# One attention job for both heads of a pair, and score and state products that alternate between row halves

## The chip, the core and the metric

One core of a Trainium2 chip runs the whole program. The metric is the device time of one execution in microseconds (us). TensorE (PE) does the matrix products from on-chip memory into the PSUM banks; VectorE (DVE), ScalarE (ACT) and GpSimd (POOL) do everything else; SyncE (SP) issues most transfers. Each engine runs its own instructions in the order in which the program wrote them, and engines wait for each other by semaphores.

## The reference, cut to what matters

Two decoder layers over 256 tokens and a width of 2048. Each layer projects the input, runs four groups of heads side by side (A: an RWKV-7 recurrence; B: stick-breaking attention; C: dilated window attention; D: differential attention), projects back, and then does a SwiGLU feed-forward block.

```
for l in range(DEPTH):
    p = h @ w_proj
    y_a = rwkv7_time_mix(r_a, k_a, v_a, ...)          # 8 heads of 64, a scan over tokens
    y_b = stick_breaking_attention(q_b, k_b, v_b)     # 8 heads of 64
    y_c = dilated_attention(q_c, k_c, v_c, rel_tab_c) # 8 heads of 64
    y_d = differential_attention(q_d, k_d, v_d, ...)  # 4 heads, each with two score maps of 64
    x = x + g1 * (concat(y_a, y_b, y_c, y_d) @ w_out[l])
    x = x + g2 * swiglu(adaLN(x))
```

In B and C a score map is `q @ k^T` with 64 terms per sum, over two blocks of 128 queries; in D each head has two such maps, subtracted after their softmax. In A the recurrence is computed in 8 chunks of 32 tokens; each chunk needs products of a running state with the chunk's rows.

## The kernel before

The program is written out once, by a planner in Python. The big projections run as "quads": weights come in by DMA as `raw`, ScalarE rounds them to `hi`, VectorE makes the rest `lo = raw - hi`, and each weight tile takes three products (`hi` with `hh`, `hi` with `hl`, `lo` with `hh`). After every few products of a quad the planner calls `tick`, which lets the jobs that are due write some instructions. So the PE queue is a stream of projection products into which pieces of attention and of the recurrence are put, and it is fixed when the program is built.

Attention jobs are Python generators that give way at each `yield`. In B (`stick`) and C (`dilated`) there is one job per head, 8 per group and layer; at most `width` = 3 of them are open at once. In D (`diff`) there is one job per head, up to 4 open, and it makes its two score maps one after the other. Two heads, 2j and 2j+1, share a tile: `q[j]` and `k[j]` hold head 2j in partitions 0 to 63 and head 2j+1 in partitions 64 to 127, so the two heads' score products use the two halves of TensorE's rows. `scores` makes one head's map with a product of 128 queries by 128 keys and one of 128 by 256. These products are in fp32, and the profile shows two records for each.

All small products write into four PSUM banks (`P`, names `m...`). A job takes banks with `bank` and gives them back to the planner with `drop` when the instructions that read them are written; in the run, the next writer of a bank waits for a semaphore until they are done. The recurrence (`rwkv`, higher priority) holds two banks, `XY`, for four chunks at a time, and takes one more for each of its other products. In each chunk but the first `state_part` is called twice: eight products with 64 rows, four for `e` = 0 (partitions 0 to 63, bank `XY[0]`) and four for `e` = 1 (partitions 64 to 127, bank `XY[1]`).

All instructions go through one helper, so the profile puts them on L180; tile names tell them apart: `qk` the q and k tiles, `S` with `kq` the state products, `aT` with `v` the value products, `consts` with `be` or `e` the transposes of the attention matrix, `sa`, `TT`, `tm` and `ab` the other products of the recurrence, and `q<-...` the projections.

Of the kernel before, what the change touches and what calls it, by code (L numbers as in the profile page):

```python
# [10 lines left out]
AF = mybir.ActivationFunctionType  # L11
ALU = mybir.AluOpType
# [12 lines left out]
NEG = -1e30  # L25
# [143 lines left out]
class Engine:  # L169


    def __init__(self, k, name, eng):
        self.k, self.ename, self.eng = k, name, eng
# [22 lines left out]


class Job:
    def __init__(self, gen, ready=0.0, prio=5):
        self.gen, self.ready, self.prio = gen, ready, prio  # L200
        self.t0 = self.made = ready


# [7 lines left out]
class Kern:  # L211
# [120 lines left out]
    def C(self, name):  # L332
        o, w = CONST[name]
        return self.consts[:, o:o + w]
# [149 lines left out]
    def tick(self, force=False):  # L484
        if self.lows and self.lows[0][5] <= self.clock["tensor"] + self.cfg.get("la", 0):
            self.lower()
        self.ada_pump()
        now = self.clock["tensor"]
        while sum(j.prio == 5 for j in self.active) < self.width and self.jobs:
            self.active.append(self.jobs.popleft())  # L490
            self.active[-1].t0 = now
        for j in list(self.active):
            if j.ready <= now and (j.prio < 2 or force or max(self.clock["vector"], self.clock["scalar"]) < now + self.cfg.get("jg", 1e9)):
                if not self.step(j):
                    self.active.remove(j)
        if force:
            self.clock["tensor"] += 200.0

    def add(self, g, prio=5):
        j = Job(g, self.clock["tensor"], prio)  # L500
        if prio < 5:
            self.active.append(j)
            self.active.sort(key=lambda x: x.prio)
        else:
            self.jobs.append(j)
# [436 lines left out]
    def rwkv(self, l, A):  # L942
        nc = self.nc
        C = self.C
        tt, stt = nc.vector.tensor_tensor, nc.vector.scalar_tensor_tensor
        lo, k, v = A["lo"], A["k"], A["v"]
# [25 lines left out]
        pss = yield from self.bank()  # L972
# [54 lines left out]
        for c in range(8):  # L1027
# [4 lines left out]
                sa0, sa = self.T2(n="sa0"), self.T2(n="sa")  # L1032

            def state_part(col, which, Sx):
                for e in range(2):
                    es = slice(64 * e, 64 * e + 64)
                    for j in range(4):
                        nc.tensor.matmul(XY[e][P, col + j * 64:col + j * 64 + 64], kq[j][es, c, which, :],
                                         Sx[es, j * 64:j * 64 + 64], start=j == 0, stop=False, skip_group_check=True)

# [114 lines left out]
                self.ys[j] = R["yo"][j]  # L1155


    def scores(self, G, h, ps):
        j, e = divmod(h, 2)
        es = slice(64 * e, 64 * e + 64)  # L1160
        q, k = G["q"][j], G["k"][j]
        self.nc.tensor.matmul(ps[:, 0:128], q[es, 0:128], k[es, 0:128], start=True, stop=True)
        self.nc.tensor.matmul(ps[:, 128:384], q[es, 128:256], k[es, 0:256], start=True, stop=True)

    def transposed(self, att3):

# [5 lines left out]
    def A3(self, n):  # L1172
        return self.T2(n=n)[:, 0:384]

    def attend(self, G, h, aT, base):

        nc = self.nc
        G["aT"][h] = aT
        if h ^ 1 not in G["aT"]:
            return  # L1180
        j = h // 2
        o = yield from self.bank()
        for e in range(2):
            aT = G["aT"].pop(2 * j + e)
            es = slice(64 * e, 64 * e + 64)
            vs = slice((2 * j + e) * 64, (2 * j + e) * 64 + 64)
            nc.tensor.matmul(o[es, 0:256], G["v"][0][:, vs], aT[:, 0:256], start=True, stop=False)
            nc.tensor.matmul(o[es, 128:256], G["v"][1][:, vs], aT[:, 256:384], start=False, stop=True)
# [5 lines left out]
    def stick(self, G, h):  # L1194
        nc = self.nc
        C = self.C
        ps = yield from self.bank()
        self.scores(G, h, ps)
        om, be = (self.T2(n=n)[:, 0:387] for n in ("om", "be"))
        nc.gpsimd.memset(om[:, 128:387:258], 0.0)  # L1200
        nc.gpsimd.memset(om[:, 257:258], 1.0)
        om3 = om.rearrange("p (b k) -> p b k", k=129)
        be3 = be.rearrange("p (b k) -> p b k", k=129)
        ps3 = ps[:, 0:384].rearrange("p (b k) -> p b k", k=128)
        nc.scalar.activation(om3[:, :, 0:128], ps3, AF.Sigmoid, scale=-1.0)
        nc.scalar.activation(be3[:, :, 0:128], ps3, AF.Sigmoid)
        self.drop()
        yield
        for t3, fill in ((om3, 1.0), (be3, 0.0)):
            d = t3[:, 0:3:2, 0:128]  # L1210
            nc.gpsimd.affine_select(d, d, [[0, 2], [-1, 128]], ALU.is_gt, fill, base=0, channel_multiplier=1)
        yield
        nc.vector.tensor_tensor_scan(om[:, ::-1], om[:, ::-1], C("sent")[:, ::-1], 1.0, ALU.mult, ALU.add)

        s1 = bass.AP(tensor=om.tensor, offset=om.offset + 1, ap=[list(om.ap[0]), [129, 3], [1, 128]])
        nc.vector.tensor_tensor(be3[:, :, 0:128], be3[:, :, 0:128], s1, ALU.mult)
        yield
        att3 = be3[:, :, 0:128]
        pt = yield from self.transposed(att3)
        aT = self.A3("aT")  # L1220
        nc.scalar.activation(aT[:], pt[:, 0:384], AF.Copy)
        self.drop()
        yield
        yield from self.attend(G, h, aT, 4)

    def load_bias(self, hb):
        t = self.T(n="bias")
# [5 lines left out]
    def softmax_parts(self, ps, bt):  # L1233

        nc = self.nc
        e = self.A3("e")
        m, s = self.small(2, "m"), self.small(2, "sm")
        for b, (a0, a1, b0) in enumerate(((0, 128, 128), (128, 384, 0))):
            nc.vector.tensor_tensor_reduce(e[:, a0:a1], ps[:, a0:a1], bt[:, b0:256], 1.0, 2 * NEG, ALU.add, ALU.max,
                                           m[:, b:b + 1])  # L1240
        nc.vector.tensor_scalar(m, m, -1.0, None, ALU.mult)
        self.drop()
        yield
        for b, (a0, a1) in enumerate(((0, 128), (128, 384))):
            nc.scalar.activation(e[:, a0:a1], e[:, a0:a1], AF.Exp, bias=m[:, b:b + 1], accum_out=s[:, b:b + 1])
        yield
        nc.vector.reciprocal(s, s)
        return e, s

    def scaled(self, a, s, key, l):  # L1250
        if self.cfg.get(key, 0) & (1 << l):
# [1 line left out]
        else:  # L1253
            self.nc.vector.tensor_scalar(a, a, s, None, ALU.mult)

    def dilated(self, l, G, h):
        nc = self.nc
        bt = self.load_bias(h)
        yield
        ps = yield from self.bank()  # L1260
        self.scores(G, h, ps)
        e, s = yield from self.softmax_parts(ps, bt)
        for b, (a0, a1) in enumerate(((0, 128), (128, 384))):
            self.scaled(e[:, a0:a1], s[:, b:b + 1], "na", l)
        yield
        pt = yield from self.transposed(e[:].rearrange("p (b k) -> p b k", k=128))
        aT = self.A3("aT")
        nc.scalar.activation(aT[:], pt[:, 0:384], AF.Copy)
        self.drop()
        yield  # L1270
        yield from self.attend(G, h, aT, 8)

    def diff(self, l, G, h):
        nc = self.nc
        es = []
        bt = self.load_bias(8 + h)
        yield
        for c in range(2):
            ps = yield from self.bank()
            self.scores(G, 2 * h + c, ps)  # L1280
            es.append((yield from self.softmax_parts(ps, bt)))
        (e0, s0), (e1, s1) = es
        nc.vector.tensor_scalar(s1, s1, self.lam[:, l:l + 1], None, ALU.mult)
        for b, (a0, a1) in enumerate(((0, 128), (128, 384))):
            self.scaled(e1[:, a0:a1], s1[:, b:b + 1], "nd", l)
# [136 lines left out]
    def layer(self, l, rstd):  # L1422
# [47 lines left out]
        for g in GROUPS:  # L1470
# [14 lines left out]
            def evv(q, G, g, sp=None):  # L1485
                for hf in range(2):
                    t = self.T2(n="v")
                    if sp:
                        nc.vector.tensor_tensor(t[:], q[hf], sp[hf][:], ALU.add)
                    else:  # L1490
                        nc.scalar.activation(t[:], q[hf], AF.Copy)
                    G["v"].append(t)
                    yield
                if g == "B":
                    for h in range(8):
                        self.add(self.stick(G, h))
                elif g == "C":
                    for h in range(8):
                        self.add(self.dilated(l, G, h))
                else:  # L1500
                    self.width = self.cfg.get("dw", 4)
                    for h in range(4):
                        self.add(self.diff(l, G, h))
            q = self.quad("q" + g, hs, "ch")
# [301 lines left out]
```

## Time and profile before

| | |
|---|---|
| time, median of 3 runs | 2706.76 us (2697.99 to 2708.77) |
| the profiled execution's own time | 2684.77 us |
| its span in the trace | 2683.1 us |
| TensorE busy | 2617.4 us, 98% of the span |
| VectorE, ScalarE busy | 67%, 42% |
| attention and recurrence, layer 0 | about 270 to 545 us of the span |
| attention and recurrence, layer 1 | about 1585 to 1870 us |

The profile is of one execution. A record of TensorE lasts from its start until its result is out, so records that follow each other overlap; what one piece of work costs the PE queue is read from its start to the start of the next piece.

### The profile page before, as it was taken

What the parts mean: (1) busy time and instruction counts of PE and PEld (TensorE: products, weight loads), DVE (VectorE), ACT (ScalarE), POOL (GpSimd) and SP (SyncE); (2) the same over time, 40 slices, a digit from 0 to 9 for tenths busy, and PEclk for the clock granted to TensorE, in tenths of its full rate; (3) what the DMA queues carried; (4) which work ended last, traced back from release to release, by engine and by line L of the source; (5) the groups of instructions that cost most, each with busy time, mean ns of one, the idle gap of its engine ahead of it and who ended that gap; (6) DMA issues with size and microseconds to landing.
All of it is one profiled execution on the core that took longest, in us unless ns stands there. A gap on an engine that the chain in (4) does not pass through costs nothing.

```text
span 2683.1 us, 43006 instructions
## 1 busy us (share of the span) xinstructions
PE 2617.4 (98%) x17446; PEld 2312.8 (86%) x17446; DVE 1806.6 (67%) x2922; ACT 1118.2 (42%) x1575; POOL 109.2 (4%) x208
## 2 busy tenths in 40 slices
PE   7999999999999999999999999999999999999998
PEld 5888887887898898898899988888888988988987
DVE  6667885659887778855577987686755554544555
ACT  2315543314434444434455443355544344344343
POOL 0001200000000000000020011000100000000001
PEclk9999999999999999999999999999999999999999
DMA  9895675787988888855566766575455555555553
GB/s 353 308 369 203 203 257 187 247 333 288 339 337 315 315 321 324 319 195 188 189 250 243 279 236 235 197 290 201 156 198 179 188 189 188 186 190 188 179 191 120
DMA packets 133609, 648.70 MB, mean 242 GB/s; under 512 B 17685, under 2 KB 23853, under 8 KB 86177
## 3 DMA queue, kind: packets, MB, share of 16 engines
q1 hardware_dynamic: 126306, 632.66, 64.7%
q0 software_dynamic: 6528, 12.25, 1.5%
q8 instruction: 136, 2.23, 0.3%
q10 hardware_dynamic: 576, 1.05, 0.1%
q14 instruction: 63, 0.52, 0.1%
HBM read 640.61 MB, written 7.62 MB: 242 GB/s over the span
## 4 chain that ended last, share of the span: by engine, by line
PE 90%; DVE 5%; DMA 3%; ACT 1%; issue 1%; SPq 0%; POOL 0%; DVEq 0%; ACTq 0%; POOLq 0%
PE q L180 74%; PE m L180 15%; DMA ar<-wada 2%; DVE ar L180 1%; DVE lo L180 1%; DVE x L180 1%; DMA raw<-wst 1%; DMA x<-xt 0%; ACT hi L180 0%; PE st L180 0%; DVE rstd L180 0%; DVE out L180 0%; ACT sh L180 0%; DVE iv L180 0%; DVE xt L180 0%
## 5 line engine op out<-in xcount | busy, mean ns | idle before, releaser
L180 DVE TENSOR_TENSOR lo<-raw,hi 128x1024 fp32r<-128x1024 f32 (+1 forms) x742 | 904.7, 1226 | 538.0 <-ACT hi L180 530.8
L180 ACT ACTIVATE hi<-raw 128x1024 fp32r<-128x1024 f32 (+1 forms) x742 | 779.9, 1057 | 952.2 <-PE q L180 781.6
L180 DVE SCALAR_TENSOR_TENSOR ar<-ar,cond 128x1024 f32<-128x1024 f32 x384 | 464.2, 1221 | 46.3 <-DMA ar<-wada 45.8
L180 PE MATMUL q<-hi,hh 128*128 128x512 f32 x1456 | 456.5, 395 | 6.8 <-ACT hh L180 6.8
L180 PE MATMUL q<-lo,hh 128*128 128x512 f32 x1456 | 454.6, 394 | 0.0
L180 PE MATMUL q<-hi,hl 128*128 128x512 f32 x1456 | 452.1, 392 | 0.0
L180 PEld LDWEIGHTS q<-hi,hl 128*128 128x128 f32 x1456 | 275.2, 189 | 58.6 <-DVE hl L180 0.3
L180 PEld LDWEIGHTS q<-hi,hh 128*128 128x128 f32 x1456 | 271.7, 189 | 62.2 <-ACT hh L180 7.6
L180 PEld LDWEIGHTS q<-lo,hh 128*128 128x128 f32 x1456 | 272.7, 189 | 57.5 <-issue 0.5
L180 PE MATMUL q<-ah,hi 128*128 128x256 f32 x1344 | 216.8, 284 | 0.0
L180 PE MATMUL q<-ah,lo 128*128 128x256 f32 x1344 | 216.4, 284 | 0.0
L180 PE MATMUL q<-al,hi 128*128 128x256 f32 x1344 | 216.3, 283 | 0.0
L180 PEld LDWEIGHTS q<-ah,hi 128*128 128x128 f32 x1344 | 185.9, 192 | 0.6
L180 PEld LDWEIGHTS q<-al,hi 128*128 128x128 f32 x1344 | 185.5, 192 | 0.0
L180 PEld LDWEIGHTS q<-ah,lo 128*128 128x128 f32 x1344 | 185.5, 192 | 0.0
L180 PE MATMUL q<-hh,lo 128*128 128x256 f32 (+1 forms) x1040 | 178.1, 291 | 6.1 <-DVE lo L180 6.0
L180 PE MATMUL q<-hh,hi 128*128 128x256 f32 (+1 forms) x1040 | 178.6, 291 | 5.1 <-ACT hh L180 3.4
L180 PE MATMUL q<-hl,hi 128*128 128x256 f32 (+1 forms) x1040 | 171.7, 285 | 0.0
L180 PEld LDWEIGHTS q<-hh,hi 128*128 128x128 f32 (+1 forms) x1040 | 145.4, 192 | 15.6 <-issue 7.1
L180 PEld LDWEIGHTS q<-hh,lo 128*128 128x128 f32 (+1 forms) x1040 | 145.3, 193 | 14.7 <-DVE lo L180 7.4
L180 PEld LDWEIGHTS q<-hl,hi 128*128 128x128 f32 (+1 forms) x1040 | 145.3, 193 | 0.1
L180 POOL TENSOR_TENSOR sq<-sq,sq 128x256 f32<-128x256 f32 x44 | 35.1, 797 | 1713.0 <-ACT sq L180 1710.5
(243 smaller groups left out, 2542.0 us busy)
## 6 DMA issues: line engine op xcount, KB each, us to landing
raw<-wst SPq DMA_DIRECT2D x369, 1024.0 KB, 4.9
ar<-wada SPq DMA_DIRECT2D x384, 512.0 KB, 6.6
whole<-wst SPq DMA_DIRECT2D x64, 512.0 KB, 7.8
x<-xt SPq DMA_DIRECT2D x32, 128.0 KB, 4.1
bias<-bskew POOLq DMA_DIRECT2D x24, 128.0 KB, 5.1
bskew<-bscr POOLq DMA_DIRECT2D x4, 576.0 KB, 12.7
xd<-x POOLq DMA_DIRECT2D x16, 128.0 KB, 6.9
x<-xd SPq DMA_DIRECT2D x16, 128.0 KB, 4.0
```

The costliest lines, as they stand in the source:

```text
L180: return f(*a, **kw)
```

## The change

There is now one job for the two heads of a pair. It takes two banks at once (`bank(2)`), and `scores` writes the four products in the order: head 2j and head 2j+1 with 128 keys, then head 2j and head 2j+1 with 256 keys. Each later step does both heads before it gives way, and gives back both banks together. In `attend` the two transposes follow each other in one job, and the value products alternate between the two heads as well. `diff` makes its two score maps in this way. `state_part` has its loops swapped, so that `e` alternates inside `j`. A job now has a share: 2.0 in B, 1.5 in C and 1.0 in D, and jobs are opened while the sum stays within `width`, which is 3 (and 3 instead of 4 in D): one pair open in B, two in C, three heads in D.

```diff
-        while sum(j.prio == 5 for j in self.active) < self.width and self.jobs:
+        while self.jobs and sum(j.share for j in self.active if j.prio == 5) + self.jobs[0].share <= self.width:
             self.active.append(self.jobs.popleft())
...
             def state_part(col, which, Sx):
-                for e in range(2):
-                    es = slice(64 * e, 64 * e + 64)
-                    for j in range(4):
+                for j in range(4):
+                    for e in range(2):
+                        es = slice(64 * e, 64 * e + 64)
                         nc.tensor.matmul(XY[e][P, col + j * 64:col + j * 64 + 64], kq[j][es, c, which, :],
                                          Sx[es, j * 64:j * 64 + 64], start=j == 0, stop=False, skip_group_check=True)
...
-    def scores(self, G, h, ps):
-        j, e = divmod(h, 2)
-        es = slice(64 * e, 64 * e + 64)
+    def scores(self, G, j, pss):
+
         q, k = G["q"][j], G["k"][j]
-        self.nc.tensor.matmul(ps[:, 0:128], q[es, 0:128], k[es, 0:128], start=True, stop=True)
-        self.nc.tensor.matmul(ps[:, 128:384], q[es, 128:256], k[es, 0:256], start=True, stop=True)
+        for a0, a1, n in ((0, 128, 128), (128, 256, 256)):
+            for e in range(2):
+                es = slice(64 * e, 64 * e + 64)
+                self.nc.tensor.matmul(pss[e][:, a0:a0 + n], q[es, a0:a1], k[es, 0:n], start=True, stop=True)
...
+    def attend(self, G, j, att, base):
+
+        nc = self.nc
+        aTs = []
+        for e in range(2):
+            pt = yield from self.transposed(att[e])
+            aT = self.A3("aT")
+            nc.scalar.activation(aT[:], pt[:, 0:384], AF.Copy)
+            self.drop()
+            aTs.append(aT)
+            yield
         o = yield from self.bank()
...
+    def stick(self, G, j):
         nc = self.nc
         C = self.C
-        ps = yield from self.bank()
-        self.scores(G, h, ps)
...
+        pss = yield from self.bank(2)
+        self.scores(G, j, pss)
...
+    def dilated(self, l, G, j):
+        bts = [self.load_bias(2 * j + e) for e in range(2)]
+        yield
+        pss = yield from self.bank(2)
+        self.scores(G, j, pss)
...
-        for c in range(2):
-            ps = yield from self.bank()
-            self.scores(G, 2 * h + c, ps)
-            es.append((yield from self.softmax_parts(ps, bt)))
-        (e0, s0), (e1, s1) = es
+        pss = yield from self.bank(2)
+        self.scores(G, h, pss)
+        (e0, s0), (e1, s1) = yield from self.softmax_parts(pss, [bt, bt])
...
                 if g == "B":
-                    for h in range(8):
-                        self.add(self.stick(G, h))
+                    for j in range(4):
+                        self.add(self.stick(G, j), share=2.0)
                 elif g == "C":
-                    for h in range(8):
-                        self.add(self.dilated(l, G, h))
+                    for j in range(4):
+                        self.add(self.dilated(l, G, j), share=1.5)
                 else:
-                    self.width = self.cfg.get("dw", 4)
+                    self.width = self.cfg.get("dw", 3)
```

The instructions are the same before and after, on TensorE 15439 products and transposes in both; their order differs, and ScalarE has 32 loads of a function table before and 36 after. Three places on TensorE show the new order.

The first is layer 0, group B, heads 4 and 5 (tiles `qk_1938` and `qk_1747`). Before, each head is written into the projection by its own job:

```order
L180 MATMUL m_2462<-consts,be_2230 128x128 x3
L180 MATMUL m_2468<-qk_1938,qk_1747 128x128
L180 MATMUL m_2468<-qk_1938,qk_1747 128x256
L180 MATMUL q_2287<-hh_465,lo_2290 128x256 x4
L180 MATMUL q_2287<-hh_501,hi_2289 128x256 x4
L180 MATMUL q_2287<-hl_516,hi_2289 128x256 x4
L180 MATMUL q_2287<-hh_501,lo_2290 128x256 x4
L180 MATMUL m_2498<-qk_1938,qk_1747 128x128
L180 MATMUL m_2498<-qk_1938,qk_1747 128x256
L180 MATMUL q_2287<-hh_565,hi_2338 128x256 x4
```

In the changed program the same four products stand together, and they stand later, in the next quad:

```order
L180 MATMUL q_2711<-hi_2669,hh_421 128x512 x2
L180 MATMUL q_2711<-hi_2669,hl_433 128x512 x2
L180 MATMUL m_2817<-qk_1938,qk_1747 128x128
L180 MATMUL m_2818<-qk_1938,qk_1747 128x128
L180 MATMUL m_2817<-qk_1938,qk_1747 128x256
L180 MATMUL m_2818<-qk_1938,qk_1747 128x256
L180 MATMUL q_2711<-lo_2670,hh_421 128x512 x2
```

So two insertions of one head each became one insertion of two heads with two banks. Over both layers the 48 heads stand in 36 groups before and in 22 after, of which 20 hold one pair and 2 hold two pairs.

The second place is one call of `state_part` in layer 0; `m_3547` and `m_3548` are the two banks of `XY`, one for each row half. Before:

```order
L180 MATMUL m_3547<-S_3639,kq_1869 32x64
L180 MATMUL m_3547<-S_3639,kq_1876 32x64
L180 MATMUL m_3547<-S_3639,kq_2327 32x64
L180 MATMUL m_3547<-S_3639,kq_2353 32x64
L180 MATMUL m_3548<-S_3639,kq_1869 32x64
L180 MATMUL m_3548<-S_3639,kq_1876 32x64
L180 MATMUL m_3548<-S_3639,kq_2327 32x64
L180 MATMUL m_3548<-S_3639,kq_2353 32x64
```

The same call in the changed program, where the banks are `m_3474` and `m_3475`:

```order
L180 MATMUL m_3474<-S_3574,kq_1869 32x64
L180 MATMUL m_3475<-S_3574,kq_1869 32x64
L180 MATMUL m_3474<-S_3574,kq_1876 32x64
L180 MATMUL m_3475<-S_3574,kq_1876 32x64
L180 MATMUL m_3474<-S_3574,kq_2309 32x64
L180 MATMUL m_3475<-S_3574,kq_2309 32x64
L180 MATMUL m_3474<-S_3574,kq_2334 32x64
L180 MATMUL m_3475<-S_3574,kq_2334 32x64
```

The products are the same eight; the row half now changes with each of them.

The third place is layer 0, group C, while the recurrence holds its two banks. Before, one head at a time is put in, with one bank, and the recurrence's product with `TT` and its update (`tm`, bank `m_3622`) follow:

```order
L180 MATMUL m_3565<-qk_2852,qk_2390 128x256
L180 MATMUL q_3366<-hh_565,hi_3417 128x256 x4
L180 MATMUL q_3366<-hl_634,hi_3417 128x256 x4
L180 MATMUL m_3588<-sa_3549,TT_3456 32x64 x8
L180 MATMUL q_3366<-hh_565,lo_3418 128x256 x4
L180 MATMUL m_3605<-qk_2852,qk_2390 128x128
L180 MATMUL m_3605<-qk_2852,qk_2390 128x256
L180 MATMUL q_3366<-hh_793,hi_3417 128x256 x4
L180 MATMUL q_3366<-hl_846,hi_3417 128x256 x4
L180 MATMUL m_3622<-tm_1708 64x64 x8
```

In the changed program two pairs, with two banks each, stand around the product with `TT`:

```order
L180 MATMUL m_3965<-qk_2746,qk_2357 128x256
L180 MATMUL m_3966<-qk_2746,qk_2357 128x256
L180 MATMUL q_3872<-lo_3619,hh_256 128x512 x2
L180 MATMUL q_3872<-hi_3678,hh_298 128x512 x2
L180 MATMUL q_3872<-hi_3678,hl_309 128x512 x2
L180 MATMUL m_4001<-sa_3476,TT_3365 32x64 x8
L180 MATMUL m_4011<-qk_2748,qk_2359 128x128
L180 MATMUL m_4012<-qk_2748,qk_2359 128x128
L180 MATMUL m_4011<-qk_2748,qk_2359 128x256
L180 MATMUL m_4012<-qk_2748,qk_2359 128x256
L180 MATMUL q_3872<-lo_3679,hh_298 128x512 x2
L180 MATMUL m_4034<-tm_1708 64x64 x8
```

With `XY` these five allocations ask for more than the four banks that there are, so each must wait until an earlier one has been read. Six of the 24 pairs are written while `XY` is held, two in layer 0 and four in layer 1; in D of each layer the third head's two maps are written right behind the second's (in layer 1 with four projection products between), when the first two heads hold all four banks.

## Rows read from the trace of the kernel before

**Rows 1.** The page, part 4: the chain that ended last, by engine.

```profile
PE 90%; DVE 5%; DMA 3%; ACT 1%; issue 1%; SPq 0%; POOL 0%; DVEq 0%; ACTq 0%; POOLq 0%
```

**Rows 2.** Busy us (and count) of PE, PEld, DVE, ACT, POOL; then clock, DMA.

```profile
270.00:545.00 275.00, 270.44 (x2388) 230.93 (x2388) 200.00 (x490) 113.58 (x246) 24.20 (x51) 0.98 0.66 228
...
1585.00:1870.00 285.00, 276.29 (x2479) 245.01 (x2480) 209.85 (x459) 134.88 (x269) 20.56 (x42) 0.97 0.63 226
```

**Rows 3.** TensorE timeline from 355 us: start, length with drain, instruction, count.

```profile
355.28 0.92 PE L180 MATMUL m<-qk,qk 64*128 64x128 f32 x4
356.13 0.74 PE L180 MATMUL q<-hh,hi 128*128 128x256 f32 x4
356.71 0.63 PE L180 MATMUL q<-hl,hi 128*128 128x256 f32 x4
357.27 0.93 PE L180 MATMUL m<-qk,qk 64*128 64x128 f32 x8
358.13 0.51 PE L180 MATMUL q<-hh,lo 128*128 128x256 f32 x2
```

**Rows 4.** TensorE timeline, two score maps among the output products, layer 0.

```profile
503.18 1.57 PE L180 MATMUL m<-qk,qk 64*128 64x128 f32 x8
504.68 1.13 PE L180 MATMUL q<-y,whole 128*128 128x256 f32 x4
```

**Rows 5.** TensorE timeline, first three heads of group B, layer 0.

```profile
274.31 1.57 PE L180 MATMUL m<-qk,qk 64*128 64x128 f32 x12
275.81 0.74 PE L180 MATMUL q<-hh,hi 128*128 128x256 f32 x4
```

**Rows 6.** TensorE timeline, two heads of opposite halves in layer 1, group C.

```profile
1712.69 1.67 PE L180 MATMUL m<-qk,qk 64*128 64x128 f32 x8
1714.28 0.39 PE L180 MATMUL q<-hh,lo 128*128 128x256 f32 x1
```

**Rows 7.** TensorE busy on the q and k tiles, four stretches, summed.

```profile
sum 390.00, PE 38.56; mean PE 9.64
```

**Rows 8.** TensorE timeline, projection followed by transposes.

```profile
286.79 0.64 PE L180 MATMUL q<-hl,hi 128*128 128x256 f32 x4
287.27 0.49 PE L180 MATMUL m<-consts,be 128*128 128x128 f32 x3
```

**Rows 9.** TensorE timeline, one state call and what follows it.

```profile
398.26 0.88 PE L180 MATMUL m<-S,kq 64*32 64x64 f32 x16
399.07 1.08 PE L180 MATMUL m<-tm,ab 32*32 32x64 f32 x16
400.08 0.75 PE L180 MATMUL q<-hh,hi 128*128 128x256 f32 x4
```

**Rows 10.** TensorE timeline, small products into alternating column halves.

```profile
392.20 0.63 PE L180 MATMUL m<-sa,tm 32*64 32x64 f32 x16
392.77 0.29 PE L180 MATMUL m<-tm,ab 32*32 32x64 f32 x2
```

**Rows 11.** TensorE timeline, value products of one head pair.

```profile
402.99 0.88 PE L180 MATMUL m<-aT,v 128*64 128x256 f32 x8
403.79 0.55 PE L180 MATMUL m<-consts,e 128*128 128x128 f32 x3
```

**Rows 12.** The page, part 6: bias loads, count, size, us to landing.

```profile
bias<-bskew POOLq DMA_DIRECT2D x24, 128.0 KB, 5.1
```

**Rows 13.** VectorE timeline: one head's scores read in group C, and the next instruction.

```profile
386.99 0.29 DVE L180 CUSTOM_DVE_ANT_0 e<-m,bias 128x128 f32<-128x128 f32 x1 [1.02 <-PE m L180]
...
387.20 0.42 DVE L180 CUSTOM_DVE_ANT_0 e<-m,bias 128x256 f32<-128x256 f32 x1
...
387.74 1.22 DVE L180 SCALAR_TENSOR_TENSOR ar<-ar,cond 128x1024 f32<-128x1024 f32 x1
```

**Rows 14.** ScalarE timeline: the second of two reads of a head, group B.

```profile
275.70 0.49 ACT L180 ACTIVATE be<-m 128x384 f32<-128x384 f32 x1
```

**Rows 15.** Busy time in a stretch at the lower clock.

```profile
1719.20:1722.60 3.40, 3.40 (x27) 3.07 (x25) 3.36 (x9) 0.00 (x0) 0.00 (x0) 0.50 0.94 290
```

More of the change, by code (lines that the diff above doesn't have):

```diff
@@ L198, with __init__ @@
 class Job:
-    def __init__(self, gen, ready=0.0, prio=5):
-        self.gen, self.ready, self.prio = gen, ready, prio
+    def __init__(self, gen, ready=0.0, prio=5, share=1.0):
+        self.gen, self.ready, self.prio, self.share = gen, ready, prio, share
         self.t0 = self.made = ready
@@ L497, in tick, with add @@
             self.clock["tensor"] += 200.0
-    def add(self, g, prio=5):
-        j = Job(g, self.clock["tensor"], prio)
+    def add(self, g, prio=5, share=1.0):
+        j = Job(g, self.clock["tensor"], prio, share)
         if prio < 5:
@@ L1173, in A3 @@
         return self.T2(n=n)[:, 0:384]
-    def attend(self, G, h, aT, base):
+    def attend(self, G, j, att, base):
         nc = self.nc
[L1178 to L1181, printed above, removed]
-        o = yield from self.bank()
[L1183 to L1188, printed above, removed]
+        aTs = []
[6 more added lines that the diff above has]
+            yield
+        o = yield from self.bank()
+        for b, (a0, a1, o0) in enumerate(((0, 256, 0), (256, 384, 128))):
+            for e, aT in enumerate(aTs):
+                es = slice(64 * e, 64 * e + 64)
+                vs = slice((2 * j + e) * 64, (2 * j + e) * 64 + 64)
+                nc.tensor.matmul(o[es, o0:256], G["v"][b][:, vs], aT[:, a0:a1], start=b == 0, stop=b == 1)
         y = self.T(n="y")
@@ L1192, in attend @@
         self.ys[base + j] = y
-    def stick(self, G, h):
+    def stick(self, G, j):
         nc = self.nc
         C = self.C
-        ps = yield from self.bank()
-        self.scores(G, h, ps)
[L1199 to L1207, printed above, removed]
+        pss = yield from self.bank(2)
+        self.scores(G, j, pss)
+        att, oms = [], []
+        for e in range(2):
+            om, be = (self.T2(n=n)[:, 0:387] for n in ("om", "be"))
+            nc.gpsimd.memset(om[:, 128:387:258], 0.0)
+            nc.gpsimd.memset(om[:, 257:258], 1.0)
+            om3 = om.rearrange("p (b k) -> p b k", k=129)
+            be3 = be.rearrange("p (b k) -> p b k", k=129)
+            ps3 = pss[e][:, 0:384].rearrange("p (b k) -> p b k", k=128)
+            nc.scalar.activation(om3[:, :, 0:128], ps3, AF.Sigmoid, scale=-1.0)
+            nc.scalar.activation(be3[:, :, 0:128], ps3, AF.Sigmoid)
+            oms.append((om, om3))
+            att.append(be3[:, :, 0:128])
+        self.drop(2)
@@ L1208, in stick @@
         yield
-        for t3, fill in ((om3, 1.0), (be3, 0.0)):
-            d = t3[:, 0:3:2, 0:128]
-            nc.gpsimd.affine_select(d, d, [[0, 2], [-1, 128]], ALU.is_gt, fill, base=0, channel_multiplier=1)
+        for e in range(2):
+            for t3, fill in ((oms[e][1], 1.0), (att[e], 0.0)):
+                d = t3[:, 0:3:2, 0:128]
+                nc.gpsimd.affine_select(d, d, [[0, 2], [-1, 128]], ALU.is_gt, fill, base=0, channel_multiplier=1)
         yield
-        nc.vector.tensor_tensor_scan(om[:, ::-1], om[:, ::-1], C("sent")[:, ::-1], 1.0, ALU.mult, ALU.add)
@@ L1215, in stick @@
-        s1 = bass.AP(tensor=om.tensor, offset=om.offset + 1, ap=[list(om.ap[0]), [129, 3], [1, 128]])
-        nc.vector.tensor_tensor(be3[:, :, 0:128], be3[:, :, 0:128], s1, ALU.mult)
-        yield
[L1218 to L1224, printed above, removed]
+        for e in range(2):
+            om = oms[e][0]
+            nc.vector.tensor_tensor_scan(om[:, ::-1], om[:, ::-1], C("sent")[:, ::-1], 1.0, ALU.mult, ALU.add)
+            s1 = bass.AP(tensor=om.tensor, offset=om.offset + 1, ap=[list(om.ap[0]), [129, 3], [1, 128]])
+            nc.vector.tensor_tensor(att[e], att[e], s1, ALU.mult)
@@ L1226, in load_bias @@
+        yield
+        yield from self.attend(G, j, att, 4)
     def load_bias(self, hb):
@@ L1231, in load_bias, with softmax_parts @@
         return t
-    def softmax_parts(self, ps, bt):
+    def softmax_parts(self, pss, bts):
         nc = self.nc
[L1236 to L1242, printed above, removed]
+        es, ms, ss = [], [], []
+        for ps, bt in zip(pss, bts):
+            e = self.A3("e")
+            m, s = self.small(2, "m"), self.small(2, "sm")
+            for b, (a0, a1, b0) in enumerate(((0, 128, 128), (128, 384, 0))):
+                nc.vector.tensor_tensor_reduce(e[:, a0:a1], ps[:, a0:a1], bt[:, b0:256], 1.0, 2 * NEG, ALU.add, ALU.max,
+                                               m[:, b:b + 1])
+            nc.vector.tensor_scalar(m, m, -1.0, None, ALU.mult)
+            es.append(e)
+            ms.append(m)
+            ss.append(s)
+        self.drop(2)
         yield
-        for b, (a0, a1) in enumerate(((0, 128), (128, 384))):
-            nc.scalar.activation(e[:, a0:a1], e[:, a0:a1], AF.Exp, bias=m[:, b:b + 1], accum_out=s[:, b:b + 1])
+        for e, m, s in zip(es, ms, ss):
+            for b, (a0, a1) in enumerate(((0, 128), (128, 384))):
+                nc.scalar.activation(e[:, a0:a1], e[:, a0:a1], AF.Exp, bias=m[:, b:b + 1], accum_out=s[:, b:b + 1])
         yield
-        nc.vector.reciprocal(s, s)
-        return e, s
+        for s in ss:
+            nc.vector.reciprocal(s, s)
+        return list(zip(es, ss))
     def scaled(self, a, s, key, l):
@@ L1254, in scaled @@
             self.nc.vector.tensor_scalar(a, a, s, None, ALU.mult)
-    def dilated(self, l, G, h):
-        nc = self.nc
-        bt = self.load_bias(h)
+    def dilated(self, l, G, j):
+        bts = [self.load_bias(2 * j + e) for e in range(2)]
         yield
-        ps = yield from self.bank()
[L1261 to L1264, printed above, removed]
-        yield
[L1266 to L1271, printed above, removed]
+        pss = yield from self.bank(2)
+        self.scores(G, j, pss)
+        att = []
+        for e, s in (yield from self.softmax_parts(pss, bts)):
+            for b, (a0, a1) in enumerate(((0, 128), (128, 384))):
+                self.scaled(e[:, a0:a1], s[:, b:b + 1], "na", l)
+            att.append(e[:].rearrange("p (b k) -> p b k", k=128))
+        yield
+        yield from self.attend(G, j, att, 8)
     def diff(self, l, G, h):
         nc = self.nc
-        es = []
         bt = self.load_bias(8 + h)
         yield
-        for c in range(2):
-            ps = yield from self.bank()
-            self.scores(G, 2 * h + c, ps)
-            es.append((yield from self.softmax_parts(ps, bt)))
-        (e0, s0), (e1, s1) = es
+        pss = yield from self.bank(2)
+        self.scores(G, h, pss)
+        (e0, s0), (e1, s1) = yield from self.softmax_parts(pss, [bt, bt])
         nc.vector.tensor_scalar(s1, s1, self.lam[:, l:l + 1], None, ALU.mult)
```

## The prediction

> **What bounds the kernel now.** I read the shares first: TensorE is busy for 98% of the span, and the chain that ended last runs through it for 90% [rows 1]. So time that leaves TensorE's queue leaves the kernel, unless a new wait takes its place. The change touches two stretches, one per layer. TensorE is idle there for 275.00 - 270.44 = 4.6 us and 285.00 - 276.29 = 8.7 us [rows 2], so it is the bound there too. Next I read TensorE's own timeline, and price each piece from its start to the start of the next one, since the lengths overlap.
>
> **Score products.** A lone score map has four records and costs 356.13 - 355.28 = 0.85 us; at 357.27 eight records, two maps of opposite row halves that happened to be neighbours, cost 358.13 - 357.27 = 0.86 us [rows 3]. The second map is free. Two neighbours of the same half cost 504.68 - 503.18 = 1.50 us [rows 4], so it is the half that matters. Three maps, the first two of opposite halves, cost 275.81 - 274.31 = 1.50 us [rows 5], as if they were two. Going through the timeline I count 26 lone maps (26 x 0.85 = 22.1 us), six neighbours of one half and two such triples (8 x 1.50 = 12.0), the pair (0.9), and one pair of opposite halves that did not overlap (1714.28 - 1712.69 = 1.59) [rows 6]: 36.6 us for 48 maps in 36 groups. Their busy time is 38.56 us [rows 7], a little more, because it holds each group's drain. After the change there are 24 pairs at 0.86: 20.6 us. That is 16.0 us less.
>
> Each group also costs at its entry: four projection products take 287.27 - 286.79 = 0.48 us ahead of transposes [rows 8], but 357.27 - 356.71 = 0.56 us ahead of scores [rows 3]. There are 36 - 22 = 14 groups fewer at 0.08 us: 1.1 us less.
>
> **State products.** One call costs 399.07 - 398.26 = 0.81 us for 16 records [rows 9]. The 16 records behind it, which all use the same 32 rows, cost 400.08 - 399.07 = 1.01 us [rows 9]: so the two halves of a call overlap a little already, where the second half's records come up before the first half's are through. The nearest row in which every product changes its part of the array has 16 records into alternating column halves, at 392.77 - 392.20 = 0.57 us [rows 10]. Here rows alternate, not columns, but row halves overlap as fully [rows 3]. There are 28 calls (two layers, seven chunks, two calls): 28 x (0.81 - 0.57) = 6.7 us. Bounds: nothing, if a call overlaps already as far as it can, and 28 x 0.81 / 2 = 11.3 us, if its time halved. I take 6.5 us, by rows 10.
>
> **What costs nothing.** The value products of two heads write opposite column halves, and their eight records cost 403.79 - 402.99 = 0.80 us already [rows 11], less than the four of a lone score map; alternating them gives nothing more. The transposes stay. The bias loads of a pair in C are issued on GpSimd's queue one behind the other, as its job opens, and land within 5.1 us [rows 12]; what hides them is the projection ahead of the scores, and late they would delay the readers, not TensorE, by about that once per pair at most. Four more table loads on ScalarE are hidden, since it is busy for 113.58 of 275 us [rows 2]; unhidden they would be late roundings of weights, priced with the waits.
>
> **What is added: waits for banks.** A pair takes two banks and gives them back when both maps are read. VectorE reads one map in C from 386.99 to 387.20 + 0.42 = 387.62, 0.63 us, and the instruction behind it is one of 1.22 us [rows 13]; ScalarE reads one in B with two instructions of 0.49 us [rows 14], 0.98 us at most. The second map's bank is free one such read later than the first's. Where `XY` holds the other two banks, the next small product must wait for it, and behind that product stands the projection. The pair in rows 6 lost 1.59 - 0.86 = 0.73 us in such a place. In the changed order there are six pairs under `XY`, and two third heads in D: eight places. Below, nothing: some have several us of projection behind them. Above: 0.98 us for the second map and 1.22 us of an instruction ahead of it, 2.2 us, for all eight: 17.6 us. I take 0.5 us each, a little under rows 6, because not all meet: 4 us. The Trainium skill speaks against the change here: "TensorEngine Tiling (Array Packing)", section Performance Considerations (PSUM Bottleneck), says that tiling speeds up TensorE but not the reading of PSUM, which may become the bottleneck. The loss in rows 6 agrees with it in kind; taken as the rule for all eight places it would leave the first rival's 2700 us.
>
> **Sum.** 16.0 + 1.1 + 6.5 = 23.6 us gained, 4 us lost: 19.6 us less. The profiled execution goes from 2684.77 to about 2665 us. It lies 22 us below the median of the timed runs, 2706.76 us, and below the lowest of them; nothing in the trace says that the gain would scale with that, so I take it off the median: **2687 us**, 0.7% less. A difference under 0.5%, 13.5 us, is about what a measurement of this kernel can't tell from no change; faster means under 2693.
>
> **Rivals.**
> - *The banks take half of it back.* At 2.2 us for each of the eight places the gain is 23.6 - 17.6 = 6 us: 2701 us. At half of that it is 14.8: 2692. For it: rows 6, and a VectorE that is busy for 200 of 275 us [rows 2], so that reads will often find it taken. Against it: in the changed order there is projection between most pairs and the next small product. Chance 0.18, centred on 2697.
> - *Records overlap only in the order of the queue.* A second map of the same half adds 1.50 - 0.85 = 0.65 us [rows 3, 4], so its records take about 0.11, 0.11, 0.21 and 0.21 us. Were a product to start only after all those ahead of it, a pair would run in five steps, in which only the middle three hold a record of each half: 0.11 + 0.11 + 0.21 + 0.21 + 0.21 = 0.85 us, and 0.20 us of entry and exit that a lone map has too: 1.05 us. 24 such pairs are 25.2 us, 11.4 less than now. With 4 us on the state products, 1.1 at entries and 4 of waits the gain is 12.5 us: 2694. Against it: the four products of each map in rows 3 stood one map behind the other, and overlapped fully. Chance 0.05. The Trainium skill, "TensorE: Matmul & The Clock Gate", section Part 3: Packing small matmuls, says that matmuls start and end strictly in the order of the queue. By that rule the pair of rows 3 could not cost 0.86 us; the trace disagrees.
> - *The change doesn't do what it says.* If the second bank of a pair is regularly free later than the first, every pair looks like rows 6: 24 x 1.59 = 38.2 us, 1.6 more than now. Then 6.5 + 1.1 - 1.6 - 4 = 2 us are left: 2705 us. It would take such a wait in most pairs, and 18 of the 24 stand where `XY` is not held. Chance 0.03.
> - *The recurrence falls behind: slower.* A pair's reads stand ahead of the small copies for which each chunk of the recurrence waits. Two layers of eight chunks with two such hops, each 2.2 us late, are 70 us; at 0.74 us a hop (23.6 us) the gain is gone, and at 1.2 us (37 us) the kernel is slower by over 0.5%. Midway between that and 70, at 54 us, it takes 2737 us. For it: in these stretches VectorE has little room. Against it: only six pairs meet the recurrence's chunks. Chance 0.04.
>
> **How the numbers follow.** The forecast has the remaining 0.70, with a range of its own from 2680 to 2692: without new waits it is 2706.8 - 23.6 = 2683. TensorE's clock adds to both ends: in short stretches such as the one at 1719 us, in which the engine was busy throughout, the granted clock is 0.50, the lower level of 1.2 GHz [rows 15]; 3.4 us there do 1.7 us of full-speed work, and two such stretches more or fewer are 3.4 us. I take 2675 to 2700: it holds the forecast with most of the state products' upper bound, the second rival and most of the first, and leaves out the last two. Faster: the forecast and a little of the first rival, 0.73. Slower: 0.04. The rest, 0.23, is no change that can be told.
>
> **What would show it.** Right: the score maps stand in 22 groups, a lone pair costs 0.86 us, and all of them take about 22 us of busy time; a state call costs 0.57 us; TensorE's idle time in the two stretches grows by some 4 us, at small products behind a pair that wait for ScalarE or VectorE. Wrong: pairs at 1.1 us or more, state calls still at 0.81 us, or over 10 us of new idle time there. What would spoil the number without touching these steps is a clock that is low for longer, or runs in which the kernel before no longer takes 2707 us.

## The result, and the profile after

The changed kernel takes 2663.9 us (median of 4 runs, 2661.55 to 2673.95) beside 2707.64 us for the kernel before on the same chip (4 runs, 2697.99 to 2708.77): 0.9853 of the time, 95% interval 0.9819 to 0.9888. It is faster, by more than I forecast: 2687 us was the number and 2675 the low end. The profiled execution takes 2661.86 us, where the working said about 2665; its span is 2660.1 us, 23.0 us less than before.

How much of this belongs to the change can't be read off one pair of medians, since executions of one kernel differ by their mean granted clock. Where it matters I therefore give span x mean granted clock as well, a "time at full clock": 2660.1 x 0.986 = 2622.9 us for the profiled execution.

What bounds the kernel has not changed. The page, part 4, the chain that ended last, by engine (it answers to [rows 1]):

```profile
PE 90%; DVE 4%; DMA 3%; ACT 1%; issue 1%; SPq 0%; DVEq 0%; ACTq 0%
```

TensorE's time outside its busy time in the two stretches of [rows 2] was 4.6 + 8.7 = 13.3 us. After, it is 7.7 + 3.8 = 11.5 us. Busy time in these windows (columns as in [rows 2]):

```profile
270.00:545.00 275.00, 267.30 (x2406) 230.17 (x2405) 198.75 (x488) 113.42 (x240) 23.00 (x53) 0.96 0.67 234
...
1585.00:1870.00 285.00, 281.21 (x2658) 254.58 (x2657) 216.45 (x467) 145.83 (x285) 18.94 (x41) 0.98 0.66 237
```

The first pair of group B, where [rows 5] had three maps. TensorE timeline:

```profile
274.59 0.93 PE L180 MATMUL m<-qk,qk 64*128 64x128 f32 x8
275.44 0.74 PE L180 MATMUL q<-hh,hi 128*128 128x256 f32 x4
276.02 0.64 PE L180 MATMUL q<-hl,hi 128*128 128x256 f32 x4
276.49 0.28 PE L180 MATMUL q<-hh,lo 128*128 128x256 f32 x1
```

A pair costs 275.44 - 274.59 = 0.85 us, as forecast by [rows 3]. The 48 maps stand in 22 groups. From start to next start these take 22.4 us in all (36.6 before): 16 lone pairs at 0.86, one at 0.93 (at a granted clock of 1.00; its second map starts 0.08 us behind its first), two groups of two pairs at 1.51, and, not in the forecast's term, three pairs that cost 1.60 as in [rows 6]. One of the three:

```profile
424.80 1.05 PE L180 MATMUL m<-sa,TT 32*32 32x64 f32 x16 [0.25 <-DVE m L180]
425.78 0.48 PE L180 MATMUL m<-qk,qk 64*128 64x128 f32 x2
426.53 0.92 PE L180 MATMUL m<-qk,qk 64*128 64x128 f32 x6 [0.27 <-ACT sa L180]
427.38 1.14 PE L180 MATMUL q<-lo,hh 128*128 128x512 f32 x2
429.13 1.12 PE L180 MATMUL m<-tm 32*64 32x64 f32 x16 [0.60 <-DVE m L180]
```

The first map has its bank, and the second waits until ScalarE has read `sa` out of the other one. With two records done, the remaining six no longer find a partner for all of their time: 427.38 - 425.78 = 1.60 us.

A state call (it answers to the first line of [rows 9]), TensorE timeline:

```profile
394.16 0.64 PE L180 MATMUL m<-S,kq 64*32 64x64 f32 x16
394.73 1.08 PE L180 MATMUL m<-tm,ab 32*32 32x64 f32 x16
395.73 0.50 PE L180 MATMUL q<-hh,lo 128*128 128x256 f32 x2
```

394.73 - 394.16 = 0.57 us, where it was 0.81; the 16 records behind it, not touched, still cost 395.73 - 394.73 = 1.00 us. All 28 calls take 16.3 us, 23.4 before.

The new wait. TensorE's waits over the whole span: us in total, times, longest:

```profile
PE m L180 <- DVE m L180: 6.7, 4, 5.5
PE q L180 <- DVE lo L180: 5.1, 4, 2.7
PE m L180 <- ACT aT L180: 0.6, 1, 0.6
PE m L180 <- ACT sa L180: 0.5, 2, 0.3
```

Most of the first line, 5.5 of 6.7 us, is one place in layer 0. The timeline of TensorE and VectorE there:

```profile
369.09 0.93 PE L180 MATMUL m<-qk,qk 64*128 64x128 f32 x8
...
371.09 0.93 PE L180 MATMUL m<-qk,qk 64*128 64x128 f32 x8
...
371.95 0.74 PE L180 MATMUL q<-hh,lo 128*128 128x256 f32 x4
...
375.25 1.23 DVE L180 SCALAR_TENSOR_TENSOR ar<-ar,cond 128x1024 f32<-128x1024 f32 x1 [2.95 <-DMA ar<-wada]
...
376.40 1.22 DVE L180 TENSOR_TENSOR lo<-raw,hi 128x1024 fp32r<-128x1024 f32 x1
...
377.54 0.28 DVE L180 CUSTOM_DVE_ANT_0 e<-m,bias 128x128 f32<-128x128 f32 x1
...
378.23 1.06 PE L180 MATMUL m<-tm,ab 32*32 32x64 f32 x8 [5.54 <-DVE m L180]
```

Two pairs, 2 us apart, take all four banks of the small products. VectorE, which must read them, first waits 2.95 us for a load of `ar` and then works off `ar` and `lo`, which stand ahead of the reads in its queue. Its first read starts at 377.54, 6.45 us after the second pair's start, and the recurrence's next small product, with the projection behind it, stands still for 5.54 us. It is the kind of wait that the prediction described, 2.5 times as long as its upper price of 2.2 us, because a late DMA is ahead of the reads. But it is at none of the eight places that the prediction priced: `XY` is not held here. In the changed program the waiting product is the first writer of `XY` itself (`m_3474` and `m_3475`, with no state product ahead of it), and those two banks are the first pair's. The chain that ended last, in order of time (start, us, what), names the same load, 8.97 us from issue to landing where the page has 6.7 us as the median for `ar`:

```profile
366.25 8.97 DMA ar<-wada
...
376.48 1.14 DVE lo L180
```

### The profile page after: what moved, and what is told of

Same layout as the page of the kernel before. It is cut to its first block, busy times and chain, and to the rows that moved or that the text cites. A ratio compares the mean times of both kernels' runs of the same rounds, so it can differ in the third digit from the quotient of the medians.

```text
span 2660.1 us, 43002 instructions
## 1 busy us (share of the span) xinstructions
PE 2594.6 (98%) x17446; PEld 2296.8 (86%) x17446; DVE 1802.8 (68%) x2922; ACT 1121.6 (42%) x1579; POOL 107.6 (4%) x208
## 4 chain that ended last, share of the span: by engine, by line
PE 90%; DVE 4%; DMA 3%; ACT 1%; issue 1%; SPq 0%; DVEq 0%; ACTq 0%
PE q L180 75%; PE m L180 14%; DMA ar<-wada 2%; DVE ar L180 1%; DVE lo L180 1%; DVE x L180 0%; PE st L180 0%; DMA raw<-wst 0%; DMA x<-xt 0%; ACT hi L180 0%; DVE rstd L180 0%; DVE out L180 0%; ACT sh L180 0%; SPq L180 0%; ACT L180 0%
## 5 line engine op out<-in xcount | busy, mean ns | idle before, releaser
L180 PEld LDWEIGHTS q<-hh,hi 128*128 128x128 f32 (+1 forms) x1040 | 148.2, 195 | 12.4 <-issue 4.9
```

Of the source, the lines that this page charges most:

```text
L180: return f(*a, **kw)
```

## The experiments

All runs below were compared with the kernel before on their own chip. There it took 2699.11 us (23 runs, 2682.98 to 2715.83; 2653.2 us at full clock) beside the first four and 2699.67 us (20 runs; 2652.9) beside the last three. Ratios stand with their 95% intervals. The first question was the level: why the profile's 2684.77 us and the median of 2707 belonged to one kernel.

**The kernel before, unchanged.**

> The kernel before, unchanged, run again beside itself. Its timed runs took 2698 to 2709 us and its profiled execution 2685 us with a mean granted clock of 0.989; the changed kernel took 2662 to 2674 us in executions of which the list shows clocks of 0.982 to 0.987. Theory 1 (the granted clock differs between executions and carries the gap between 2685 and 2707): the executions lie on one line of time against clock, some 3 us for each 0.001 of clock as the changed kernel's do (2659.8 us of span at 0.987, 2672.2 at 0.982), so runs near 2707 us show about 0.982, and runs near 2685 about 0.989. Theory 2 (the clock has nothing to do with it; the kernel before takes 2707 us at any clock, and its profile was an odd execution): runs near 2707 us at 0.987 to 0.989. Ratio 1.00 either way.

0.9993 [0.9965, 1.0022], median 2694.04 us. Its 12 executions run from 2681.59 us at a mean clock of 0.989 to 2711.98 us at 0.981: 30 us for 0.008, some 3.8 us per 0.001 between these two, while span x clock stays between 2648 and 2659 us, 2653.6 in the mean. So the 22 us between the profile and the median that the prediction set against each other are of the size that one program shows at two clocks. The clocks of the three runs behind 2707 us are not on record; that they were low is inferred from the repeat, whose runs at 2703 to 2712 us have 0.981 to 0.982.

**The state products alone.** The kernel before, with only this:

```diff
-                for e in range(2):
-                    es = slice(64 * e, 64 * e + 64)
-                    for j in range(4):
+                for j in range(4):
+                    for e in range(2):
+                        es = slice(64 * e, 64 * e + 64)
```

> The kernel before with only the state products alternating. Theory 1 (the change gains what leaves TensorE's queue, and the rest is clock): 28 calls go from 0.81 to 0.57 us, 6.8 us less, ratio 0.9975, and in the trace the score maps and waits stay as before. Theory 2 (the state products hold more than the queue shows, since each chunk of the recurrence waits for them): more than 10 us less, with fewer waits in the two stretches.

0.9949 [0.9927, 0.9971], median 2682.30 us; at full clock 2647.7 us, 5.5 less than before (95% interval 1.7 either way; those of the differences below are 1.3 to 2.5). The 14 to 17 us of the timed runs look like theory 2, but their mean clock is 0.987 against 0.984, and the waits in the trace are not fewer: at full clock it is theory 1. A call costs 0.57 us, as in the changed kernel, and the score groups are as they were (36.6 us). TensorE timeline:

```profile
418.13 0.64 PE L180 MATMUL m<-S,kq 64*32 64x64 f32 x16
418.70 0.96 PE L180 MATMUL m<-tm,ab 32*32 32x64 f32 x14
```

**The pairs alone.** The changed kernel with the old loops in `state_part` (the diff above, reversed).

> The changed kernel with the state products in the old order (row half by row half). Theory 1: 6.8 us slower than the changed kernel and some 16 us faster than before in queue time, state calls back at 0.81 us and pairs still at 0.86 us; with the state products alone the two parts add up to the whole change, within what the clock moves. Theory 2: the parts do not add up; most of the gain of 44 us in the timed runs is in one of them.

0.9926 [0.9902, 0.9951], median 2678.65 us; at full clock 2631.3 us, 21.9 less. A lone pair costs 0.86 us in its trace, a state call 0.81 again. The parts add up: 5.5 + 21.9 = 27.4, and the whole change gives 27 to 29 us at full clock.

**Pairs one behind the other.** The changed kernel, with the four records of one head ahead of the four of the other:

```diff
-        for a0, a1, n in ((0, 128, 128), (128, 256, 256)):
-            for e in range(2):
+        for e in range(2):
+            for a0, a1, n in ((0, 128, 128), (128, 256, 256)):
```

> The changed kernel with each pair's four score products one head behind the other, as the neighbours in the kernel before stood. Theory 1 (it is enough that two heads of opposite halves are neighbours): pairs at 0.86 us still, and the same time as the changed kernel within 0.3%. Rival (only alternation lets records overlap, as a strict queue order would have it): pairs at 1.05 to 1.5 us, 22 groups x 0.2 to 0.6 = 4 to 14 us slower than the changed kernel.

0.9872 [0.9849, 0.9895], median 2661.87 us, as fast as the changed kernel. The first pair, TensorE timeline:

```profile
276.89 0.93 PE L180 MATMUL m<-qk,qk 64*128 64x128 f32 x8
277.75 0.74 PE L180 MATMUL q<-hh,hi 128*128 128x256 f32 x4
```

0.86 us again. Alternating within a pair is worth nothing that shows at the end of the kernel; that the two maps are neighbours is enough. (The two groups of two pairs cost 1.61 us here, 1.51 when alternating.) The rival of the strict queue falls, and with it, for these records, the Trainium skill's rule ("TensorE: Matmul & The Clock Gate", Part 3: Packing small matmuls) that matmuls start and end in the order of the queue: four records of the second half overlapped four of the first that stood ahead of all of them. TensorE's records in the first 0.1 us of this pair (those under way between 276.88 and 276.99 us; the last figure counts them):

```profile
276.89 0.39 PE L180 MATMUL m<-qk,qk 64*128 64x128 f32 x2
```

and of the same pair where both heads use one half, the experiment that follows (between 277.48 and 277.60 us):

```profile
277.48 0.37 PE L180 MATMUL m<-qk,qk 64*128 64x128 f32 x1
```

Two records have started in the one, one in the other. So it does not hold for these records that an engine runs its instructions in the order in which they were written.

**The same half twice.** The changed kernel, in which the second head of a pair takes the first head's q and k, so that the overlap of row halves is left out:

```diff
-                es = slice(64 * e, 64 * e + 64)
+                es = slice(0, 64)
```

> The changed kernel, but both heads of a pair compute their scores from the first head's half of q and k, so that no row halves differ (the second head's scores are not its own; everything else is computed as in the changed kernel). Jobs, banks and order stay. Theory 1 (the overlap of row halves gives 14 to 15 us, and the rest, some 8 us, comes from fewer groups and fewer waits): a pair costs 1.50 us instead of 0.86, 22 groups or 24 pairs about 14 us more in all, 2638 us at full clock: it stays 15 us below the kernel before, 7 of them by the state products. Rival (merging the jobs gains nothing by itself, and the records explain it all): 2646 us at full clock, that of the kernel with the state products alone.

0.9921 [0.9895, 0.9946], median 2679.23 us; at full clock 2634.5 us, 8.5 to 10.4 more than the changed kernel (2624.1 in its first four runs, 2626.0 in the repeat). A pair costs 278.99 - 277.48 = 1.51 us, as in [rows 4]; TensorE timeline:

```profile
277.48 1.57 PE L180 MATMUL m<-qk,qk 64*128 64x128 f32 x8
278.99 0.74 PE L180 MATMUL q<-hh,hi 128*128 128x256 f32 x4
```

All score groups take 37.4 us, 15.0 more than in the changed kernel and 0.8 more than before the change. So not all of the overlap's 15 us reaches the end. TensorE's waits for VectorE's reads are smaller when pairs are slower (waits of this kernel; 6.7 us in the changed one), and by the accounting told below all waits in the two stretches are 3.6 us less and other products 1.0 us less, which leaves some 10 us:

```profile
PE m L180 <- DVE m L180: 2.2, 3, 1.8
```

The other side is larger than theory 1 had it (15 us, 8 of them without the state products): with score products as dear as before, this kernel is still 18.4 us faster than the kernel before at full clock, of which the state products are 5.5. Some 13 us of the gain come with the merged jobs, not from the overlap: by the same accounting other products take 7.4 us less than before, and TensorE's waits 15.5 us instead of 20.9. The number of jobs open at once changed too, and no run here tells it from the merging.

**Fewer maps held at once.** Group C opened with one pair at a time, to take the 5.54 us wait away:

```diff
-                        self.add(self.dilated(l, G, j), share=1.5)
+                        self.add(self.dilated(l, G, j), share=2.0)
```

> The changed kernel with share 2.0 instead of 1.5 in group C, so that one pair is open at a time instead of two. In the changed kernel's trace the second pair's scores at 371 us filled all four banks, and TensorE then waited 5.5 us for VectorE, which had to wait for a transfer before it could read the scores. Theory 1 (the four full banks make that wait): with one pair open the recurrence finds free banks there, and TensorE's waits for VectorE behind scores fall from 6 us to under 2 us; some 4 us less at full clock, 2620. Rival (the wait is VectorE's, and comes at another place whatever is open): no change within 2 us, or slower, since the jobs of C end later.

1.0021 [0.9993, 1.0048], no faster than the kernel before; at full clock 2645.4 us, 20 us lost. The rival had the direction and the reason, that the jobs of C end later, and neither had the size. The wait aimed at is gone (the longest for `m` is 1.7 us), and larger ones came (waits, then the timeline of TensorE):

```profile
PE m L180 <- DVE e L180: 17.1, 5, 8.0
...
PE m L180 <- ACT aT L180: 6.2, 3, 3.3
...
PE m L180 <- DVE m L180: 2.2, 2, 1.7
```

```profile
500.84 0.63 PE L180 MATMUL m<-consts,yc 128*128 128x128 f32 x4 [2.48 <-DVE yc L180]
501.39 3.31 PE L180 MATMUL m<-qk,qk 64*128 64x128 f32 x16
512.74 0.47 PE L180 MATMUL m<-consts,e 128*128 128x128 f32 x1 [8.04 <-DVE e L180]
```

The jobs of C end too late; the last scores fall among the output products, where no projection is left to cover their softmax, and TensorE stands for 8.04 us. The number of open jobs alone thus moves this kernel by 20 us. The granted clock is lower as well. Span and mean granted clock of this kernel and of the repeated kernel before:

```profile
core 0: 2718.5 us, clock 0.974
```

```profile
core 0: 2686.6 us, clock 0.988
```

**The changed kernel again.**

> The changed kernel, unchanged, beside the kernel before in the same session. In the first session the kernel before took 2707.6 us and the changed one 2663.9 (ratio 0.985); in the second the kernel before took 2699 in 23 executions with a mean clock of 0.984. Span times clock, the time at full clock, is 2653 us for before and 2624 for the changed kernel. Theory 1 (the true gain is 29 us at full clock, and the rest of the 44 us in the first session was the clock that the few runs of before happened to get): ratio 0.987 to 0.990, and a mean clock within 0.002 of that of before. Rival (the change also raises the granted clock): mean clock 0.003 or more above that of before, ratio 0.985 or less.

0.9876 [0.9843, 0.9909]: 2665.34 us (2658.24 to 2671.74) against 2699.67. This is the better measure of the change: 34 us, not 44, with 20 runs of the kernel before instead of four. The kernel after has stayed (2663.9, 2665.3); the kernel before has moved. The ratio is theory 1's. The mean clock, 0.986 against 0.983, lies between the two theories.

## Why the prediction was off

The direction and the queue prices of the two products were right; the number was 23 us too high. The base of the forecast, a median of three runs, was some 8 us too high; two terms of the sum, entries and waits, were some 10 us off; the last 5 to 6 us are clock. Taken apart at full clock: I give each stretch between the starts of two neighbouring TensorE records to the first of the two, set idle time apart, and take off half of what lies at a granted clock of 0.50. The stretches are wider than in [rows 2], in the kernel before about 190 to 611 us and 1366 to 1916 us.

| Step | predicted | measured |
|---|---|---|
| score products | -16.0 | -15.0 |
| state products | -6.5 | -6.9 |
| entries, and all other products | -1.1 | -6.4 |
| waits | +4 | -1.8 |
| sum | -19.6 | -30.1 in the trace, -27 to -29 in the runs |

**Score products: right.** 22 groups, 0.86 us a pair, and 22.4 us against the 20.6 of the working (21.6 with the waits inside pairs set apart, as in the table); what is more are the three pairs that could not overlap (3 x 0.74 = 2.2 us), and the two double groups give 0.4 back. At the end of the kernel the overlap is worth less, 8.5 to 10.4 us by the run with the same half twice.

**State products: right,** with a call at the 0.57 us that [rows 10] gave. The run with this part alone shows 5.5 us, 1.7 either way, at the end of the kernel.

**Entries: the term was too small.** I priced what a group costs ahead of it and left out what it costs behind it, although the rows were there: four projection products are 0.74 us long behind scores [rows 3, 5] and 0.64 elsewhere [rows 8], and so after the change (0.74 at 275.44, 0.64 at 276.02). With 0.08 + 0.10 us the 14 groups fewer are 2.5 us, not 1.1. The other 3.9 are spread thinly: 1.0 on value products in layer 1, 0.5 on products from `sh`, a little on each kind of projection. The run with the same half twice shows about the same sum (7.4 us less), so it comes with the merged jobs; which part of the merging gives it was not separated.

**Waits: the term had the wrong sign.** At the eight places that it priced, the 4 us were about right: 0.74 us in each of the three pairs that could not overlap, and some 1.1 us of other waits there, 0.60 of it at 429.13. What it left out is a ninth place, two pairs written just ahead of the recurrence's own two banks, which cost 5.54 us, more than twice its bound for any place (2.2); and that a changed order also removes waits. TensorE's waits for `lo` fell from 8.5 to 5.1 us in the span, and in layer 1 those for `hi` (2.0 us), `be` (1.3) and `aT` (1.3) went: over these stretches, one per layer, 8.5 + 12.4 = 20.9 us of waits became 10.9 + 8.2 = 19.1.

**The level: the step that failed outright.** I took the gain off the median of 2706.76 us, since "nothing in the trace says that the gain would scale with" the 22 us between profile and median. The question was a different one: whether those 22 us would be there again. They are what a lower clock makes of this kernel, as far as the repeat shows. It runs from 2681.59 to 2711.98 us, its clock with it, and the medians of 23 and 20 runs are 2699 and 2700. The prediction had named this itself as what would spoil the number. Taken off 2699 the same 19.6 us give 2680, and the two terms above some 10 us more: 2670. The last 5 to 6 us are clock as well: the changed kernel's runs average 0.985 to 0.986, the kernel before 0.983 to 0.985. Whether the change raised it or it was drawn so, these runs don't settle.

**The signs.** Of the prediction's own signs of being right, the groups (22), their time (22.4 us) and the state call (0.57 us) came; the fourth did not, since idle time in the two stretches fell from 13.3 to 11.5 us instead of growing by 4.

**The rivals.** Banks that take half back: the mechanism is real, with some 3.3 us at the eight places and 5.54 us at the ninth; it did not decide, as other waits went. The strict queue: fallen, by the pairs one behind the other. "It doesn't do what it says": three pairs of 24 look like [rows 6]. The recurrence falling behind did not show, but for the 5.54 us. That reads of PSUM may take over as the bound, the rule that I weighed from the Trainium skill ("TensorEngine Tiling (Array Packing)", Performance Considerations, PSUM Bottleneck), agrees with this trace only in kind at that one place (5.54 us, of which the reads first stood behind 2.95 us of a late load), not as a rule for the stretches: VectorE is busy for 198.75 of 275 us.

## What to carry to other kernels

Records of opposite row halves overlap when they are neighbours in the queue, so first make them neighbours; alternating them paid here where a half had eight records in a row (a state call, 0.81 to 0.57 us), and not where it had four (a pair, 0.86 either way; its records are larger, so the count alone is not shown to decide). Price a small group at both its ends, and ask of a changed order which old waits it takes away, not only which it adds. Before a gain is taken off a median, look at the clock of the runs behind it, and build on the span times the clock when the runs are few.

## What I had not expected of the hardware

One kernel on one core ran anywhere from 2681.59 us at a mean granted clock of 0.989 to 2711.98 at 0.981, a spread of 1.1%, about what this change is worth. And a wait may cost more than its length. Busy time and granted clock (columns as in [rows 2]) from the last 1.9 us of the 5.54 us wait on:

```profile
376.30:383.10 6.80, 4.87 (x30) 4.70 (x31) 6.61 (x27) 1.69 (x3) 0.56 (x1) 0.50 0.91 331
```

TensorE had been idle since about 372.7, the clock stands at its lower level of 1.2 GHz for 6.8 us, and the 4.87 us of work in it would have taken about half of that at 2.4 GHz (an estimate: four projection products take 392.04 - 391.18 = 0.86 us in a later stretch at the lower level, 0.48 elsewhere). The traces of the pairs alone, of the pairs one behind the other and of the changed kernel again have the same wait, of 4.0 to 5.0 us, and 6.8 us at the lower level that begin within it. That the wait brings the lower level about is not shown: the clock also falls where TensorE was busy throughout [rows 15].
